# A decoder layer on one core: weight buffers laid out by release, and the order of gate tail, evictions, splits and sums changed

## The chip, the cores and the metric

The kernel runs on one core of a Trainium2 chip. The metric is the device time of one execution in microseconds; a kernel's time is the median of its runs. The engines are TensorE (PE, matmuls), VectorE (DVE), ScalarE (ACT), GpSimd (POOL) and SyncE (SP, which here only issues DMAs); each takes its instructions in program order and stops at one whose operands or buffers are not ready.

## The reference

One decoder layer in float32 for 512 tokens of width 2048. Three groups of heads read one input projection, their outputs are normalised per head, gated and projected, and an MLP with a squared ReLU follows:

```python
proj = rms_norm(h) @ w_in
(gq, gk, gv, gg, ga, fq, fk, fv, fg, ff, mq, mg) = split(proj)
...   # gated linear attention, forgetting attention, attention to a memory
o = rms_norm(concat([gla_o, fox_o, mem_o]))          # per head
gate = concat([silu(gg), sigmoid(fg), sigmoid(mg)])
h = h + (o * gate) @ w_out                           # 2048 x 2048
u = relu(rms_norm(h) @ w_up)                         # 2048 x 8192
h = h + (u * u) @ w_down                             # 8192 x 2048
```

## The kernel before, in words

**Matmuls.** Each float32 operand is split in a high and a low part of a narrower format (the high part by a cast on ACT, the low one by a subtraction on DVE), and each product is three matmuls: high by high, high by low, low by high (`mm3`, L170 to L172). The projections of the first half (`project`, L261) go in pairs of 128 rows of the weight, `kp` 0 to 7, through the double buffers raw, hi and lo of pool `wp`. The last four groups are the gates gg0, gg1, fg and mg (L645 on).

**The gate tail.** After a gate's projection, for each of four banks: z by DVE (L656), log-sigmoid as Abs, Exp, Ln on ACT and one DVE operation (L352 to L355), Exp on ACT (L658), and the product with the heads, DVE, L661. `block_sums` (L611) then makes the sums s1 to s4 of the quarters of the result. These seven blocks are the left operands: `left0` (A11) and `left3` (S1) are split at once into buffers of their own; the others go through DRAM tiles `oo` (POOL's DMAs, L673) and are fetched by SP (L606) and split (L601, L602) once the attention's buffers are given back. `left4` is S2, `left5` S3, `left6` S4, `left1` A12, `left2` A22.

**The second half.** w_out is two multiplies (out0, out1), w_up eight (up0 to up7) and w_down eight (dn0_0 to dn3_1). Each is a seven-product scheme of Strassen and Winograd: products p in the order 1, 5, 6, 3, 7, 2, 4, each of four steps q. A product's left operand is one of the seven blocks, its right operand a block of the weight or a difference of blocks. Raw weights come in 1 MB tiles `raw` from a ring of six (`wr`, loaded by SP, L710); differences are taken in place on DVE (L717); for each q ACT casts a half tile (L755) and DVE makes the low part (L756), both into a ring of four `hl` tiles (`wm`). Twelve matmuls use one `hl` tile. In out0 the first eight steps are taken as 10, 11, 12, 50, 51, 52, 13, 53 (first digit the product).

**Banks and evictions.** Products 1, 6, 7 and 4 add to one pair of PSUM banks, 5 and 3 to another; after each product the bank is read out before the next product adds to it. In w_out, DVE adds it to a tile x, loaded by SP (L795, L806); in w_up and w_down ACT copies it (z L942, m L987) or DVE adds. Blocks of the new h are turned by PE (L828) and scaled by ACT (L831), and `operands` makes their sums (hs, L615 to L621), which are the left operands of w_up: through DRAM tiles `uo` for the first half, directly split for the second.

**What sets the order.** The code is written in one sequence, and a scheduler orders each engine's instructions by priority; `tc.high_priority(offset=...)` moves what stands in it ahead. Splits and differences of weights have an offset of 3000 (`AHEAD`), block loads of x 300; evictions and the gate tail have none. Rings of buffers decide when a load may start: a tile of a ring waits for the last reader of whatever lay in its place.

## Time and profile before

| | us |
|---|---|
| median of 3 runs | 2209.56 (2207.89 to 2209.83) |
| profiled execution, its time | 2212.55 |
| profiled execution, its span | 2210.8 |
| PE busy | 2151.7 (97%) |
| DVE busy | 1534.9 (69%) |
| ACT busy | 1076.9 (49%) |
| GpSimd busy | 115.2 (5%) |

The span runs from the first to the last instruction on the engines; 1.75 us of the profiled execution lie around it. Busy shares are means over the whole program. The projections and the attention fill the first 741 us, w_out runs to about 945 us, w_up to about 1600 and w_down to the end. The views used are the busy shares of the page, the windows view (busy time, granted clock and DMA rate of a stretch), the timeline of one engine (start, duration, operation, idle time before it and what released it) and the list of waits.

### The profile page before, as it was taken

How to read it: one execution, taken by the hardware profiler on the slowest of the kernel's cores; microseconds unless marked ns; L12 is line 12 of the kernel's file. 1: busy time of each engine (PE TensorE's matmuls, PEld its weight loads, DVE VectorE, ACT ScalarE, POOL GpSimd, SP SyncE). 2: the span in 40 equal slices, each digit the busy share in tenths (PEclk: the TensorE clock that was granted, in tenths of full speed). 3: DMA queues.
4: the chain of work that ended last, by engine and by line, in shares of the span. 5: the costliest groups of instructions: out<-in, count | busy, mean ns of one | idle time of the engine just before them, and what ended most of it. 6: DMA issues, size and time to landing. Idle time of an engine off the chain costs nothing. (4 is left out here: it accounts for less than half of the span.)

```text
span 2210.8 us, 25318 instructions
## 1 busy us (share of the span) xinstructions
PE 2151.7 (97%) x9842; PEld 1750.4 (79%) x9842; DVE 1534.9 (69%) x1714; ACT 1076.9 (49%) x1469; POOL 115.2 (5%) x187
## 2 busy tenths in 40 slices
PE   8999999999999878999999999999999999999999
PEld 7777778777778657878888888888878888788787
DVE  5264775247576678787687677778868868767775
ACT  5233232345554445555555545555645546546443
POOL 2000000000001001000000000000010000000000
PEclk9999999999999989999999999999999999999999
DMA  5222112225134365614534433534676777668554
GB/s 192 83 77 76 50 56 80 73 91 171 60 106 145 140 221 213 233 68 157 176 130 150 171 143 126 189 143 182 237 211 187 221 200 210 190 196 267 149 189 133
DMA packets 72131, 336.61 MB, mean 152 GB/s; under 512 B 8377, under 2 KB 10425, under 8 KB 49994
## 3 DMA queue, kind: packets, MB, share of 16 engines
q1 hardware_dynamic: 53162, 267.35, 34.8%
q0 software_dynamic: 18848, 67.64, 11.3%
q8 instruction: 77, 1.26, 0.2%
q14 instruction: 44, 0.36, 0.0%
HBM read 263.13 MB, written 71.83 MB: 152 GB/s over the span
## 5 line engine op out<-in xcount | busy, mean ns | idle before, releaser
L755 ACT CAST hl_up<-raw_up 128x1024 fp32r<-128x1024 f32 x224 | 235.8, 1053 | 283.3 <-PE acc_up L172 258.9
L756 DVE TENSOR_TENSOR hl_up<-raw_up,hl_up 128x1024 fp32r<-128x1024 f32 x224 | 273.2, 1222 | 137.1 <-ACT hl_up L755 136.8
L755 ACT CAST hl_dn<-raw_dn 128x1024 fp32r<-128x1024 f32 x224 | 235.5, 1053 | 240.1 <-PE acc_dn L172 185.9
L756 DVE TENSOR_TENSOR hl_dn<-raw_dn,hl_dn 128x1024 fp32r<-128x1024 f32 x224 | 270.7, 1221 | 101.1 <-ACT hl_dn L755 100.7
L717 DVE TENSOR_TENSOR raw_dn<-raw_dn,raw_dn 128x2048 f32<-128x2048 f32 x64 | 145.9, 2287 | 16.1 <-DMA raw_dn<-in_w_down_dram 15.8
L717 DVE TENSOR_TENSOR raw_up<-raw_up,raw_up 128x2048 f32<-128x2048 f32 (+1 forms) x65 | 146.4, 2253 | 2.1 <-DMA raw_up<-in_w_up_dram 1.9
L755 ACT CAST hl_out<-raw_out 128x1024 fp32r<-128x1024 f32 x56 | 58.4, 1052 | 71.6 <-PE acc_out L172 57.2
L756 DVE TENSOR_TENSOR hl_out<-raw_out,hl_out 128x1024 fp32r<-128x1024 f32 x56 | 67.8, 1222 | 32.2 <-ACT hl_out L755 32.0
L988 POOL DMA_DIRECT2D hd<-m x48 | 41.6, 874 | 508.5 <-ACT m L987 508.5
L987 ACT COPY m<-acc_dn 128x512 f32<-128x512 f32 x96 | 55.6, 584 | 8.7 <-PE acc_dn L172 8.7
L171 PE MATMUL gg<-alo_x,hi_gg 128*128 128x512 f32 x128 | 52.9, 414 | 0.0
L171 PE MATMUL acc_up<-hl_up,left0h 128*128 128x512 f32 x128 | 50.3, 393 | 1.9 <-DVE hl_up L756 1.9
L170 PE MATMUL acc_dn<-hl_dn,left4h 128*128 128x512 f32 x128 | 50.0, 390 | 2.2 <-ACT m L987 2.2
L171 PE MATMUL acc_dn<-hl_dn,left4h 128*128 128x512 f32 x128 | 50.1, 391 | 1.9 <-DVE hl_dn L756 1.9
L170 PE MATMUL gg<-ahi_x,hi_gg 128*128 128x512 f32 x128 | 51.8, 405 | 0.0
L170 PE MATMUL acc_up<-hl_up,left0h 128*128 128x512 f32 x128 | 50.7, 397 | 1.1 <-ACT hl_up L755 1.1
L171 PE MATMUL gv<-lo_gv,ahi_x 128*128 128x512 f32 x128 | 51.7, 404 | 0.0
L172 PE MATMUL gv<-hi_gv,alo_x 128*128 128x512 f32 x128 | 51.6, 403 | 0.0
L170 PE MATMUL acc_up<-hl_up,left4h 128*128 128x512 f32 x128 | 49.9, 390 | 1.6 <-ACT z L942 1.6
L172 PE MATMUL gg<-ahi_x,lo_gg 128*128 128x512 f32 x128 | 51.3, 402 | 0.0
L171 PE MATMUL acc_dn<-hl_dn,left3h 128*128 128x512 f32 x128 | 50.3, 393 | 0.9 <-DVE hl_dn L756 0.9
L170 PE MATMUL acc_up<-hl_up,left3h 128*128 128x512 f32 x128 | 50.8, 397 | 0.0
(545 smaller groups left out, 6088.2 us busy)
## 6 DMA issues: line engine op xcount, KB each, us to landing
raw_up<-in_w_up_dram SPq DMA_DIRECT2D x64, 1024.0 KB, 4.8
raw_dn<-in_w_down_dram SPq DMA_DIRECT2D x64, 1024.0 KB, 6.9
hd<-m POOLq DMA_DIRECT2D x48, 512.0 KB, 7.5
raw_out<-in_w_out_dram SPq DMA_DIRECT2D x16, 1024.0 KB, 4.9
op<-u POOLq DMA_DIRECT2D x32, 512.0 KB, 3.1
op<-s POOLq DMA_DIRECT2D x24, 512.0 KB, 2.9
raw_gv<-in_w_in_dram SPq DMA_DIRECT2D x16, 512.0 KB, 3.4
raw_mem<-in_w_mem_dram SPq DMA_DIRECT2D x16, 512.0 KB, 3.7
```

The source lines that it names most:

```text
L170: T.matmul(ps, lhsT=ah, rhs=bh, start=start, stop=False, skip_group_check=on)
L171: T.matmul(ps, lhsT=ah, rhs=bl, start=False, stop=False, skip_group_check=on)
L172: T.matmul(ps, lhsT=al, rhs=bh, start=False, stop=stop, skip_group_check=on)
L717: V.tensor_sub(dst[:, cs], a[:, cs], b[:, cs])
L755: A.copy(hi, part)
L756: V.tensor_sub(lo, part, hi.bitcast(F32))
L987: A.copy(st[:, t * 512 : t * 512 + 512], acc[t])
L988: nc.gpsimd.dma_start(dst, st.rearrange("p (t n) -> p t n", t=2), accum_op=ALU.add)
```

## The change

The weight buffers and the `hl` tiles get fixed places instead of rings: a raw tile has one of six tags, by block and half, and a group of four blocks starts one tag further on; `hl` tiles count through four tags. The last projection, mg, goes through its weight pairs in the order 0, 7, 6, ... 1, in the other pool of banks. The high part and three quarters of the low part of S2 (`left4`) get a resident pool `third`; for the first three gates it is split in place and only the last quarter goes through DRAM, into a tile `left4m`. The tail of mg, with its sums and DMAs, is put at an offset of 6000, the evictions of all products likewise (`urgent`), and the fetches of the left operands for w_out at 1000. The x tiles are loaded from `inside` at the first step of a product. The sums of `operands` for f = 0, 1 and 2 go to GpSimd. A renewed left operand is fetched one product later. The number of matmuls is the same.

The diff, cut to its core:

```diff
+    third = ctx.enter_context(tc.tile_pool(name="third", bufs=1))
...
-    def project(*groups, turned=False, first=False, bank=gbank):
-
+    def project(*groups, turned=False, first=False, bank=gbank, order=range(NK // 2)):
+
+        first_k, last_k = 2 * order[0], 2 * order[-1] + 1
...
-        for kp in range(NK // 2):
+        for kp in order:
...
+    CUT = 1536
+    high = {i: bigt([128, 2048], f"left{i}h", FR) for i in (A11, S1)}
+    low = {i: [bigt([128, 2048], f"left{i}l", FR)] for i in (A11, S1)}
+    high[S2] = third.tile([128, 2048], FR, name=f"left{S2}h")
+    low[S2] = [third.tile([128, CUT], FR, name=f"left{S2}l")]
...
-    def block_sums(a11, a12, a21, a22, temp):
+    def block_sums(a11, a12, a21, a22, temp, eng=V):
...
+        def add(dst, a, b, op):
+            eng.tensor_tensor(dst, a, b, op=op)
...
-        ps = project(group, turned=True, bank=gbank if n < 3 else abank)
+        last = n == 3
+
+        ps = project(
+            group, turned=True, bank=abank if last else gbank, order=(0, 7, 6, 5, 4, 3, 2, 1) if last else range(NK // 2)
+        )
+        finish_heads = ExitStack()
+        if last:
+            finish_heads.enter_context(tc.high_priority(offset=2 * AHEAD))
...
-            if i in left:
-                hi, lo = (halves(v[:, cs]) for v in left[i])
+            if i in (A11, S1) or i == S2 and not last:
+                hi, lo = halves(high[i][:, cs]), halves(lower(i, cs))
...
-    wm = ctx.enter_context(tc.tile_pool(name="wm", bufs=4, reuse_waits="tile"))
-    wr = ctx.enter_context(tc.tile_pool(name="wr", bufs=6, reuse_waits="tile"))
+    wm = ctx.enter_context(tc.tile_pool(name="wm", bufs=1, reuse_waits="tile"))
+    wr = ctx.enter_context(tc.tile_pool(name="wr", bufs=1, reuse_waits="tile"))
...
+    low[S2].append(ap.tile([128, 2048 - CUT], FR, name=f"left{S2}m"))
...
+    def urgent():
+        return tc.high_priority(offset=2 * AHEAD)
...
-            raw = wr.tile([128, 2048], F32, tag="raw", name=f"raw_{name}_{r}{c}{s}")
+
+            slot = {(0, 0): 0, (0, 1): 1, (1, 1): 2, (1, 0): 2}[r, c] + group
+            raw = wr.tile([128, 2048], F32, tag=f"raw{slot % 3}{s}", name=f"raw_{name}_{r}{c}{s}")
...
-                both = wm.tile([128, 2048], FR, tag="hl", name=f"hl_{name}_{p}{q}")
+                both = wm.tile([128, 2048], FR, tag=f"hl{turns['hl'] % 4}", name=f"hl_{name}_{p}{q}")
+                turns["hl"] += 1
...
-            tasks.append((0, lambda: fetch(i, cs, src)))
+            tasks.append((1, lambda: fetch(i, cs, src)))
...
-            r, c = {1: (0, 0), 2: (0, 0), 6: (0, 1), 3: (0, 1), 5: (1, 1), 7: (1, 1), 4: (1, 0)}[p]
-            if p in (1, 6, 5, 4):
-                z[r, c] = block(r, c)
-            for t in range(2):
-                v = z[r, c][:, t * 512 : t * 512 + 512]
-                V.tensor_add(v, v, acc[t])
+            r, c = WHERE[p]
+            with urgent():
+                for t in range(2):
+                    v = z[r, c][:, t * 512 : t * 512 + 512]
+                    V.tensor_add(v, v, acc[t])
...
+            parts = block_sums(
+                h0[:, :512], h0[:, 512:], h1[:, :512], h1[:, 512:], temps.get, G if f < 3 else V
+            )
...
         def inside(p, q):
+            if q == 0 and p in (1, 6, 5, 4):
+                block(*WHERE[p])
...
-        for cs in (slice(0, 1536), slice(1536, 2048)):
-            fetch(i, cs, out_op[i][:, cs])
+        for cs in (slice(0, 1536), slice(1536, 2048))[i == S2 :]:
+            with tc.high_priority(offset=1000):
+                fetch(i, cs, out_op[i][:, cs])
...
-            evict(p, acc)
+            with urgent():
+                evict(p, acc)
```

What the change moves is seen in each engine's list of instructions. On ACT, at the end of mg and the start of out0 (ee_mg is the gate tail, hl_out_10 the cast of product 1, step 0), before:

```order
L658 ACTIVATE ee_mg_5841<-ee_mg_5841 128x512
L354 ACTIVATE ee_mg_5850<-ee_mg_5850,wide 128x512
L755 CAST hl_out_10_5969<-raw_out_000_5963 128x1024
L755 CAST hl_out_11_5984<-raw_out_000_5963 128x1024
L658 ACTIVATE ee_mg_5850<-ee_mg_5850 128x512
L353 ACTIVATE ee_mg_5859<-ee_mg_5859 128x512
L755 CAST hl_out_12_5999<-raw_out_001_5965 128x1024
L354 ACTIVATE ee_mg_5859<-ee_mg_5859,wide 128x512
L670 CAST left0h<-o 128x512
L658 ACTIVATE ee_mg_5859<-ee_mg_5859 128x512
L755 CAST hl_out_50_6022<-raw_out_000_5963 128x1024
L755 CAST hl_out_51_6037<-raw_out_000_5963 128x1024
```

and now:

```order
L355 ACTIVATE ee_mg_5869<-ee_mg_5869 128x512
L702 CAST left0h<-o 128x512
L690 ACTIVATE ee_mg_5860<-ee_mg_5860 128x512
L356 ACTIVATE ee_mg_5869<-ee_mg_5869,wide 128x512
L801 CAST hl_out_10_5975<-raw_out_000_5969 128x1024
L690 ACTIVATE ee_mg_5869<-ee_mg_5869 128x512
L801 CAST hl_out_11_5992<-raw_out_000_5969 128x1024
L801 CAST hl_out_12_6007<-raw_out_001_5971 128x1024
L702 CAST left3h<-s_mg 128x512
L801 CAST hl_out_50_6030<-raw_out_000_5969 128x1024
L801 CAST hl_out_51_6047<-raw_out_000_5969 128x1024
L801 CAST hl_out_52_6062<-raw_out_001_5971 128x1024
```

The tail's activations, but for the last Exp, stand ahead of hl_out_10 now, and left3h of the last gate ahead of hl_out_50.

On DVE, in out0, around the first eviction (x_00 from bank acc_out_1; L717 and L762 are differences of raw tiles, L756 and L802 low parts), before:

```order
L756 TENSOR_TENSOR hl_out_61_6127<-raw_out_000_5963,hl_out_61_6127 128x1024
L717 TENSOR_TENSOR raw_out_011_6017<-raw_out_111_6109,raw_out_011_6017 128x2048
L756 TENSOR_TENSOR hl_out_62_6142<-raw_out_001_5965,hl_out_62_6142 128x1024
L615 TENSOR_TENSOR s_mg<-o 128x512
L621 TENSOR_TENSOR s_mg<-o 128x512
L617 TENSOR_TENSOR s_mg<-s_mg,o 128x512
L671 TENSOR_TENSOR left3l<-s_mg,left3h 128x512
L619 TENSOR_TENSOR s_mg<-o,s_mg 128x512
L806 TENSOR_TENSOR x_00_6082<-x_00_6082,acc_out_1_0_5967 128x512
L756 TENSOR_TENSOR hl_out_63_6157<-raw_out_001_5965,hl_out_63_6157 128x1024
L806 TENSOR_TENSOR x_00_6082<-x_00_6082,acc_out_1_1_5968 128x512
L806 TENSOR_TENSOR x_11_6102<-x_11_6102,acc_out_5_0_6020 128x512
```

and now:

```order
L802 TENSOR_TENSOR hl_out_52_6062<-raw_out_001_5971,hl_out_52_6062 128x1024
L802 TENSOR_TENSOR hl_out_13_6077<-raw_out_001_5971,hl_out_13_6077 128x1024
L762 TENSOR_TENSOR raw_out_000_5969<-raw_out_110_6112,raw_out_000_5969 128x2048
L762 TENSOR_TENSOR raw_out_001_5971<-raw_out_011_6025,raw_out_001_5971 128x1024
L621 TENSOR_TENSOR left4m<-left4m,left4h 128x512
L802 TENSOR_TENSOR hl_out_60_6118<-raw_out_000_5969,hl_out_60_6118 128x1024
L802 TENSOR_TENSOR hl_out_53_6095<-raw_out_001_5971,hl_out_53_6095 128x1024
L802 TENSOR_TENSOR hl_out_61_6135<-raw_out_000_5969,hl_out_61_6135 128x1024
L762 TENSOR_TENSOR raw_out_001_5971<-raw_out_111_6115,raw_out_001_5971 128x2048
L762 TENSOR_TENSOR raw_out_011_6025<-raw_out_111_6115,raw_out_011_6025 128x2048
L853 TENSOR_TENSOR x_00_5990<-x_00_5990,acc_out_1_0_5973 128x512
L853 TENSOR_TENSOR x_00_5990<-x_00_5990,acc_out_1_1_5974 128x512
```

The sums s_mg have gone ahead of this place; the eviction x_00 now stands ahead of hl_out_62, behind two differences of 128x2048.

On SP, where the x tiles of out1 are loaded (x_10 is still out0's; the next x_00, x_11 and x_01 are out1's; left0l and left3l are fetched from the sums of the new h), before:

```order
L710 DMA raw_out_111_6680<-in_w_out_dram 128x2048
L795 DMA x_10_6481<-in_x_dram 128x1024
L606 DMA left0l<-uo_5926 128x1024
L606 DMA left3l<-uo_5929 128x1024
L795 DMA x_00_6600<-in_x_dram 128x1024
L795 DMA x_11_6672<-in_x_dram 128x1024
```

and now:

```order
L753 DMA raw_out_111_6685<-in_w_out_dram 128x2048
L842 DMA x_10_6442<-in_x_dram 128x1024
L842 DMA x_00_6530<-in_x_dram 128x1024
L626 DMA left0l<-uo_5935 128x1024
L842 DMA x_11_6633<-in_x_dram 128x1024
L842 DMA x_01_6703<-in_x_dram 128x1024
L626 DMA left3l<-uo_5938 128x1024
```

x_00 of out1 stands ahead of left0l and left3l, and all its x tiles ahead of left3l.

## Rows read from the trace of the kernel before

**Rows 1.** The page: engines' shares, and low parts of w_out (busy, mean ns).

```profile
PE 2151.7 (97%) x9842; PEld 1750.4 (79%) x9842; DVE 1534.9 (69%) x1714; ACT 1076.9 (49%) x1469; POOL 115.2 (5%) x187
...
L756 DVE TENSOR_TENSOR hl_out<-raw_out,hl_out 128x1024 fp32r<-128x1024 f32 x56 | 67.8, 1222 | 32.2 <-ACT hl_out L755 32.0
```

**Rows 2.** Windows: length, busy PE, PEld, DVE, ACT, POOL; PE clock; DMA; GB/s.

```profile
700.00:750.00 50.00, 43.48 (x187) 35.19 (x186) 25.05 (x33) 23.84 (x38) 3.12 (x5) 0.95 0.35 129
750.00:800.00 50.00, 35.58 (x131) 27.60 (x131) 41.95 (x39) 21.93 (x24) 3.26 (x6) 0.81 0.60 228
800.00:850.00 50.00, 46.48 (x206) 38.19 (x206) 35.57 (x35) 25.34 (x39) 5.43 (x10) 0.97 0.63 216
850.00:900.00 50.00, 42.75 (x187) 34.96 (x187) 39.96 (x36) 21.97 (x29) 4.34 (x8) 0.93 0.44 162
...
950.00:1000.00 50.00, 45.31 (x193) 36.16 (x192) 42.96 (x47) 26.29 (x39) 0.53 (x1) 0.97 0.22 77
```

**Rows 3.** Timeline of PE: start, length, operation [idle before it and its releaser].

```profile
747.93 1.22 PE L170 MATMUL acc_out<-hl_out,left0h 128*128 128x512 f32 x2 [6.48 <-ACT hl_out L755]
...
777.55 0.80 PE L170 MATMUL acc_out<-hl_out,left3h 128*128 128x512 f32 x1 [8.05 <-ACT left3h L670]
...
789.59 0.79 PE L170 MATMUL acc_out<-hl_out,left4h 128*128 128x512 f32 x1 [6.37 <-ACT left4h L601]
...
816.88 0.59 PE L170 MATMUL acc_out<-hl_out,left5h 128*128 128x512 f32 x1 [3.52 <-DVE x L806]
...
884.00 0.77 PE L170 MATMUL acc_out<-hl_out,left4h 128*128 128x512 f32 x1 [7.25 <-DVE x L806]
...
955.58 0.50 PE L171 MATMUL acc_up<-hl_up,left0h 128*128 128x512 f32 x1 [1.94 <-DVE hl_up L756]
```

**Rows 4.** PE's waits over the span: us in total, times, longest.

```profile
PE acc_dn L171 <- DVE hl_dn L756: 2.7, 5, 0.9
PE acc_dn L170 <- ACT m L987: 2.2, 1, 2.2
...
PE ot L642 <- DVE o L638: 1.7, 1, 1.7
```

**Rows 5.** Timeline of ACT, at the start and in the middle of out0.

```profile
740.17 0.63 ACT L352 ACTIVATE ee_mg<-z_mg 128x512 f32<-128x512 f32 x1 [8.74 <-DVE z_mg L656]
...
746.85 1.98 ACT L755 CAST hl_out<-raw_out 128x1024 fp32r<-128x1024 f32 x2
...
824.25 1.05 ACT L755 CAST hl_out<-raw_out 128x1024 fp32r<-128x1024 f32 x1 [1.68 <-PE acc_out L172]
826.96 1.05 ACT L755 CAST hl_out<-raw_out 128x1024 fp32r<-128x1024 f32 x1 [1.66 <-PE acc_out L172]
```

**Rows 6.** Timeline of DVE in out0.

```profile
761.68 5.62 DVE L717 TENSOR_TENSOR raw_out<-raw_out,raw_out 128x2048 f32<-128x2048 f32 x3
...
776.17 0.68 DVE L615 TENSOR_TENSOR s_mg<-o 128x512 f32<-128x512 f32 x1
...
816.05 2.48 DVE L806 TENSOR_TENSOR x<-x,acc_out 128x512 f32<-128x512 f32 x4
```

**Rows 7.** Timeline of SP's queue: first issue, time to the last of them.

```profile
741.25 3.10 SPq L710 DMA_DIRECT2D raw_out<-in_w_out_dram  x6
744.40 35.76 SPq L795 DMA_DIRECT2D x<-in_x_dram  x3
...
877.64 1.79 SPq L795 DMA_DIRECT2D x<-in_x_dram  x3
```

**Rows 8.** DMA, 740 to 800: rate in 40 slices, one issue (KB, us to landing).

```profile
GB/s 0 87 366 426 431 426 431 431 415 431 437 396 418 208 0 0 0 0 0 0 0 0 0 0 0 30 320 147 303 374 434 406 412 221 318 391 427 397 415 128
...
oo<-s_mg POOLq DMA_DIRECT2D x3, 256.0 KB, 4.5
```

**Rows 9.** Timelines of POOL and of DVE in the attention.

```profile
274.14 1.46 POOL L459 TENSOR_TENSOR qk<-qTs,kTs 128x512 f32<-128x512 f32 x1 [40.75 <-PE lp L447]
...
274.96 1.19 DVE L444 TENSOR_TENSOR e<-e,kTs 128x512 f32<-128x512 f32 x1
```

More of the change, by code (lines that the diff above doesn't have):

```diff
@@ L591, in hybrid_layer, with lower, pieces @@
         )
-    left = {i: [bigt([128, 2048], f"left{i}{p}", FR) for p in "hl"] for i in (A11, S1)}
-    out_op = {i: dram.tile([128, 2048], F32, name=f"oo_{i}") for i in range(7) if i not in left}
+    CUT = 1536
[3 more added lines that the diff above has]
+    low[S2] = [third.tile([128, CUT], FR, name=f"left{S2}l")]
+    out_op = [dram.tile([128, 2048], F32, name=f"oo_{i}") for i in range(7)]
+    def lower(i, cs):
+        if i != S2:
+            return low[i][0][:, cs]
+        if cs.start < CUT:
+            assert cs.stop <= CUT
+            return low[i][0][:, cs]
+        return low[i][1][:, cs.start - CUT : cs.stop - CUT]
+    def pieces(i, cs):
+        if i == S2 and cs.start < CUT < cs.stop:
+            return [slice(cs.start, CUT), slice(CUT, cs.stop)]
+        return [cs]
     def split_left(i, cs, src):
-        hi, lo = (v[:, cs] for v in left[i])
-        A.copy(hi, src)
-        V.tensor_sub(lo, src, hi.bitcast(F32))
+        A.copy(high[i][:, cs], src)
+        V.tensor_sub(lower(i, cs), src, high[i][:, cs].bitcast(F32))
     def fetch(i, cs, src):
-        nc.sync.dma_start(left[i][1][:, cs].bitcast(F32), src)
+        for c in pieces(i, cs):
+            nc.sync.dma_start(lower(i, c).bitcast(F32), src[:, c.start - cs.start : c.stop - cs.start])
     def resplit(i, cs):
-        split_left(i, cs, left[i][1][:, cs].bitcast(F32))
-    def block_sums(a11, a12, a21, a22, temp):
+        for c in pieces(i, cs):
+            split_left(i, c, lower(i, c).bitcast(F32))
+    def block_sums(a11, a12, a21, a22, temp, eng=V):
         s1, s2, s4, s3 = (temp(v) for v in ("s1", "s2", "s4", "s3"))
+        def add(dst, a, b, op):
+            eng.tensor_tensor(dst, a, b, op=op)
         yield A11, a11
-        V.tensor_add(s1, a21, a22)
+        add(s1, a21, a22, ALU.add)
         yield S1, s1
-        V.tensor_sub(s2, s1, a11)
+        add(s2, s1, a11, ALU.subtract)
         yield S2, s2
-        V.tensor_sub(s4, a12, s2)
+        add(s4, a12, s2, ALU.subtract)
         yield S4, s4
-        V.tensor_sub(s3, a11, a21)
+        add(s3, a11, a21, ALU.subtract)
         yield S3, s3
@@ L685, in hybrid_layer @@
     ap = ctx.enter_context(tc.tile_pool(name="ap", bufs=1, side="right", reuse_waits="tile"))
-    wm = ctx.enter_context(tc.tile_pool(name="wm", bufs=4, reuse_waits="tile"))
-    wr = ctx.enter_context(tc.tile_pool(name="wr", bufs=6, reuse_waits="tile"))
+    wm = ctx.enter_context(tc.tile_pool(name="wm", bufs=1, reuse_waits="tile"))
+    wr = ctx.enter_context(tc.tile_pool(name="wr", bufs=1, reuse_waits="tile"))
     mp = ctx.enter_context(tc.tile_pool(name="mp", bufs=STAGES, reuse_waits="tile"))
-    for i in (S2, S4, S3, A12, A22):
-        left[i] = [ap.tile([128, 2048], FR, name=f"left{i}{p}") for p in "lh"][::-1]
+    for i in (S4, S3, A12, A22):
+        low[i] = [ap.tile([128, 2048], FR, name=f"left{i}l")]
+        high[i] = ap.tile([128, 2048], FR, name=f"left{i}h")
+    low[S2].append(ap.tile([128, 2048 - CUT], FR, name=f"left{S2}m"))
     ssq = const.tile([128, NT, 4], F32, name="ssq")
@@ L759, in multiply @@
                     j = 2 * q + kk
-                    ah, al = (a[:, j * 256 + u * 128 : j * 256 + u * 128 + 128] for a in left[OPERAND[p]])
+                    ts = slice(j * 256 + u * 128, j * 256 + u * 128 + 128)
+                    ah, al = high[OPERAND[p]][:, ts], lower(OPERAND[p], ts)
                     cs = slice(kk * 512, kk * 512 + 512)
@@ L793, in block @@
             with tc.high_priority(offset=300):
-                v = stage(f"x_{n}_{r}{c}")
-                nc.sync.dma_start(v.rearrange("p (t n) -> p t n", t=2), x[r, 2 * n + c])
-            return v
+                z[r, c] = stage(f"x_{n}_{r}{c}")
+                nc.sync.dma_start(z[r, c].rearrange("p (t n) -> p t n", t=2), x[r, 2 * n + c])
+        WHERE = {1: (0, 0), 2: (0, 0), 6: (0, 1), 3: (0, 1), 5: (1, 1), 7: (1, 1), 4: (1, 0)}
         def after(p, acc):
@@ L838, in operands @@
         def operands(f, h0, h1):
+            cs = slice(f * 512, f * 512 + 512)
             st = [stage(f"hs_{f}_{i}") for i in range(2)]
             temps = dict(s1=st[0][:, :512], s2=st[0][:, 512:], s4=st[1][:, :512], s3=st[1][:, 512:])
-            cs = slice(f * 512, f * 512 + 512)
-            for i, src in block_sums(h0[:, :512], h0[:, 512:], h1[:, :512], h1[:, 512:], temps.get):
+            parts = block_sums(
+                h0[:, :512], h0[:, 512:], h1[:, :512], h1[:, 512:], temps.get, G if f < 3 else V
+            )
+            for i, src in parts:
                 if not n:
@@ L959, in inside @@
             if (p, q) == (1, 1):
-                with tc.high_priority(offset=300):
-                    rest()
+                rest()
                 ss = const.tile([128, NT], F32, name="ss_h")
@@ L976, in after @@
             rest()
-            evict(p, acc)
+            with urgent():
+                evict(p, acc)
             renew(p, read_down(c + 1) if n and not final else None)
```

8 lines of the change are left out of this document (6 added, 2 removed).

## The prediction

> **What bounds the kernel now.** I read the page's busy shares first: TensorE (PE) works 97% of the span, the next engine (DVE) 69% [rows 1]. So a change that leaves the matmuls alone, as this one does (9,494 matmul rows on PE before and after), can only win what PE loses in gaps and at the low clock after them. Where these are, the windows view tells [rows 2]: in each stretch of 50 us, PE's busy time times the granted clock is the work it did at full speed, and what lacks to 50 is lost. 700 to 750: 50 - 43.48 x 0.95 = 8.7 us; 750 to 800: 50 - 35.58 x 0.81 = 21.2; 800 to 850: 4.9; 850 to 900: 10.2; 950 to 1000: 6.0. Together 51 us, 2.3% of the span; the rest of the w_up and w_down stages runs nearly without gaps. That is the most there is to win here.
>
> The timeline of PE in those stretches names each gap and its releaser [rows 3]: 6.48 us before the first product of w_out (the cast hl_out), 8.05 (left3h), 6.37 (left4h), 3.52 and 7.25 (evictions x), and 1.94 at the start of w_up. The list of PE's waits adds a lone 2.2 us at the w_down stage and 1.7 at the head transposes [rows 4]. What the reader is to see is that none of these is a lack of engine time: each is an order. SP issues the six 1 MB loads raw_out only at 741.25, as the last matmul of mg ends, and only then come x and left4l, 744.40 to 780.26 [rows 7]. DVE runs three block differences at 761.68 and reaches the sum s_mg, which left3h waits for, at 776.17; the four evictions at 816.05 stand in the same queue [rows 6].
>
> **A, the start of w_out.** Four casts and activations more stand ahead of hl_10 on ACT (16 where there were 12). The twelve took from 740.17 to 746.85 [rows 5], 0.557 us each, so the cast moves to 749.1 and PE's start, 1.08 behind it, from 747.93 to 750.2: 2.2 us are lost here. The loads are no longer the reason: three of the six now go out before mg's last pair of rows, and the remaining 3 MB at about 426 GB/s [rows 8] are in by 749. Then DVE decides. From the low part of q 10 (751.4) to that of q 50 it issues three 128x1024 (1.15 us each, a little under the mean of 1222 ns in [rows 1], as neighbours overlap), six 128x512 at 0.62 (a quarter of 2.48 in [rows 6]) and the three differences for 5.62 [rows 6]: 12.8 us, so PE goes on at 764.2. One q takes PE 2.71 us (two casts that each wait for PE stand that far apart, 824.25 and 826.96 [rows 5]); three of them and 2.5 us of low clock end at 760.8, which leaves a new idle of 3.4. The five q up to 53 end at 777.8. The sum s_mg and left3h are done by 756, so the gap of 8.05 is gone. q 60 adds to the bank of product 1 and waits for the eviction x_00. Ahead of that on DVE, after hl_50: six 128x1024 (6.9), three 128x2048 and one 128x1024 difference (7.7), one 128x512 and the two evictions (1.9), 16.5 us, to 780.7. Its other condition is x_00 in place, and the x loads now stand behind the left fetches on SP: left4m waits for oo of s2 (summed at 755, DMA 4.5 us [rows 8]: 759.5), then 4.75 MB at 426 GB/s are 11.7 us: 771 to 773, in time. So PE starts q 60 at 780.7 where it was 789.59 [rows 3]: **8.9 us won**. Bounds: 0, if the fetches or casts of left6 and left5, which stand ahead of hl_60 and hl_53 on ACT, come as late as left4h does now; 12, if q 60 follows q 53 without a gap.
>
> **B, the gap at 816.88.** On DVE the eviction of x_01 now stands ahead of hl_32; before, the splits up to hl_73 and two differences preceded it. PE has all of product 3 (four q, 10.8 us) before it needs the bank. The whole loss of that window goes: **4.9 us** (bounds 3.5, the idle alone, and 4.9).
>
> **C, the gap at 884.00.** x_1_00 was issued at 877.64 [rows 7], behind left3l, which waited on SP for a sum on its way through DRAM. It now stands ahead of left0l and left3l; what it waits for is a stage buffer, free when GpSimd has done the four sums of f=0. With 1.46 us for a 128x512 on GpSimd [rows 9] and the DMA issues between them I get about 850, more than 10 us ahead of need. **10.2 us**, bounds 0 (buffer late) and 10.2.
>
> **D, sums on GpSimd and the start of w_up.** Twelve sums go from DVE (0.68 us, [rows 6]) to GpSimd; the nearest row for what they cost there is the one 128x512 product on that engine, 1.46 us [rows 9]. Those of f=0 and 1 feed DRAM copies and are hidden. For f=2, four splits wait on them on ACT and DVE, ahead of the first casts hl_up: four sums now last 5.7 us instead of 2.7, so hl_up_11 may come up to 4 us later, while DVE, which sets the pace there (the 1.94 of [rows 3]), is relieved of 2.7 us. I take **0**, bounds -8 (4 us late, with as much again for the low clock and the queue behind) and +6 (the window's whole loss).
>
> At these sums the Trainium skill speaks against the change: "SBUF — State Buffer", section "Who interferes with whom", says that a DVE instruction with two SBUF inputs and a GpSimd instruction that reads SBUF exclude each other for a whole instruction. The trace agrees: while GpSimd's product ran from 274.14 to 275.60, the DVE product that began at 274.96 took 1.19 us [rows 9], 0.5 over the 0.68 of its size. By that rule the twelve sums cost DVE at most 12 x 0.5 = 6 us, which counts on PE for f=2 alone, 2 us; that would leave D's value inside its bounds.
>
> **E and F.** The eviction m of [rows 4] now precedes the next cast on ACT: **2.2 us** (bounds 0 and 2.2). The transposes ot_2 and ot_3 are issued later and may lose the 1.7 of [rows 4], but whether they meet another wait there I can't see: **0**, up to 1.7. At no cost I put S2's in-place split for the first three groups (a cast and a subtraction of 128x512 for each, under running projections), the two-piece fetch of left4 (one more DMA issue) and the ring order of the weight buffers in steady state. Their cover is the slack of a cast: four hl buffers, a cast of about 1 us and a low part of 1.2 against three q of 2.71; without it each would cost its own length at each product.
>
> **The sum.** 8.9 + 4.9 + 10.2 + 0 + 2.2 + 0 = 26.2 us. The profiled execution lies 2.99 us above the median of the runs (2212.55 and 2209.56); taken off the first it gives 2186.4, off the median 2183.4. I predict 2183.
>
> **Rivals.** *The gap only moves.* The casts of left6 and left5 wait for their fetches with hl_60 and hl_53 behind them, or x_00 comes late; A is 0 and 17.3 us remain: 2192. For it: 8 MB pass one queue in order, and DMA was full here for 14 us already [rows 8]. Against it: my times leave x_00 seven us. Chance 0.17.
> *GpSimd holds up x_1_00 and w_up.* D is -8 and C 0: 8.0 us remain, 2201.5. For it: 1.46 us where DVE takes 0.68, and the stretched 1.19 of [rows 9]. Against it: GpSimd is otherwise idle there. Chance 0.13.
> *All is covered.* q 60 follows at once (12), w_up starts without loss (6), the transposes too (1.7): 37.0 us, 2172.6. For it: both remaining gaps are 3 us by a sum of many small terms. Chance 0.17.
> *Slower.* The evictions now stand ahead of a cast at each product's end, on ACT or DVE. If the cast that is pushed back then comes too late, all 112 products of w_up and w_down pay. Today's five waits of that kind cost 2.7 us, 0.54 each [rows 4]: 60 us, and 34 more than before after the gains, 2244. It decides from 0.27 us a product, where it eats the 26 us and the 4.4 that can be measured. Against it stands the slack named above, 8.1 us for a push of 1.2. Chance 0.06.
> *It does not do what it says*, since each freed wait is followed by another at the same place: under 4.4 us, about 2208. Chance 0.04.
>
> **How the numbers follow.** The forecast (2177 to 2189) has 0.43. Faster by over 0.2%, 4.4 us, about what a measurement of this kernel can tell from no change: 0.43 + 0.17 + 0.17 and most of the GpSimd case, 0.88. Within it: 0.04 and the rest of that case, 0.06. Slower: 0.06. The range leaves out the last two cases and the ends of their neighbours: from all covered (2172.6, less the 2.7 us of small waits of w_down [rows 4]) to the GpSimd case (2201.5, and 1.4 us, B's other bound): 2169 to 2203.
>
> **What will show it.** In the new trace, PE's first q of w_out at about 750, not earlier; an idle of 3 us before q 50, released by a low part, and of 3 before q 60, released by x; no wait for left3h or left4h; no gap at products 7 of the first pair and 6 of the second (816.88 and 884.00 now); GpSimd sums of about 1.4 us, and the wait at w_up's start of about 5 us as now. I am wrong if PE waits for left6h or left5h, if x_00 lands after 780, if x_1_00 is issued after 865, or if small idles stand at every product of w_up.

## The result, and the profile after it

The changed kernel takes **2189.61 us** (median of 4 runs, 2187.03 to 2191.86), the kernel before beside it 2209.69: ratio 0.990, 95% interval 0.9869 to 0.9931, faster by 1.0%. The forecast was 2183.0 with 2169 to 2203; side and range held, and the time lies 6.6 us above the forecast. The profiled execution took 2189.32 us, with a span 23.2 us shorter than before's 2210.8. Three executions ran at a granted clock of 0.56 or 0.64 (two of the kernel called Together below, 3604 and 3609 us, and one of the last, 3128 us), and the times below leave them out. The page's shares answer to [rows 1]:

```profile
PE 2147.0 (98%) x9842; PEld 1748.0 (80%) x9842; DVE 1535.0 (70%) x1708; ACT 1076.3 (49%) x1475; POOL 132.8 (6%) x196
```

The engines do what they did, and GpSimd 17.6 us more. What changed is in the windows (length, busy PE, PEld, DVE, ACT, POOL; PE clock; DMA; GB/s), beside [rows 2]:

```profile
700.00:750.00 50.00, 41.31 (x178) 33.44 (x178) 25.56 (x34) 24.46 (x38) 2.73 (x5) 0.94 0.51 187
750.00:800.00 50.00, 45.90 (x184) 36.78 (x184) 47.57 (x43) 25.96 (x27) 3.11 (x5) 0.92 0.51 190
800.00:850.00 50.00, 50.00 (x238) 41.77 (x237) 41.28 (x33) 29.43 (x50) 17.64 (x21) 1.00 0.75 270
850.00:900.00 50.00, 48.78 (x219) 40.13 (x219) 45.05 (x40) 25.99 (x34) 6.37 (x8) 1.00 0.59 203
900.00:950.00 50.00, 43.91 (x199) 35.58 (x198) 45.10 (x42) 32.95 (x54) 8.18 (x6) 0.95 0.29 105
950.00:1000.00 50.00, 50.00 (x225) 41.41 (x225) 33.61 (x37) 25.20 (x32) 1.07 (x2) 0.98 0.46 160
```

The 9,494 matmul rows of the prediction stand in no view shown here; the page counts 9842 instructions on PE in both kernels.

Read as before (50 less busy PE times clock), the stretches lose 11.2, 7.8, 0, 1.2, 8.3 and 1.0 us: 29.5 in place of 51. The start of w_out is a little worse, 750 to 900 is nearly clean, and the start of w_up (now in 900 to 950) loses more than it did. PE's timeline names what is left, beside [rows 3]:

```profile
748.31 1.22 PE L171 MATMUL acc_out<-hl_out,left0h 128*128 128x512 f32 x2 [8.65 <-ACT hl_out L801]
...
761.64 0.73 PE L171 MATMUL acc_out<-hl_out,left0h 128*128 128x512 f32 x2 [1.36 <-ACT hl_out L801]
...
777.88 0.50 PE L171 MATMUL acc_out<-hl_out,left4h 128*128 128x512 f32 x1 [2.74 <-DVE x L853]
...
860.95 0.50 PE L172 MATMUL acc_out<-hl_out,left4h 128*128 128x512 f32 x1 [1.22 <-DVE hl_out L802]
...
940.34 0.50 PE L172 MATMUL acc_up<-hl_up,left3h 128*128 128x512 f32 x1 [1.70 <-DVE hl_up L802]
...
947.49 0.80 PE L171 MATMUL acc_up<-hl_up,left4h 128*128 128x512 f32 x1 [4.35 <-ACT z L996]
...
1590.56 0.77 PE L171 MATMUL acc_dn<-hl_dn,left4h 128*128 128x512 f32 x1 [2.65 <-ACT m L1041]
```

The waits in out0 for left3h and left4h and the gap before product 7 are gone, and of the 7.25 us before product 6 of out1, 1.22 are left, for a low part. q 60 of out0 waits 2.74 us for the eviction x_00, as forecast (3). The wait for z in up0 has grown to 4.35 us; in the kernel before it was 1.62:

```profile
973.38 0.50 PE L170 MATMUL acc_up<-hl_up,left4h 128*128 128x512 f32 x1 [1.62 <-ACT z L942]
```

Between these gaps the same matmuls stand at the same distances in both traces, so the difference in start of one matmul, taken where PE has the same work behind it in both, tells what was won up to it:

| matmul | before | after | won so far | of it here |
|---|---|---|---|---|
| mg, first | 697.76 | 695.98 | 1.8 | 1.8 (F and before) |
| out0, q 60 | 789.59 | 777.88 | 11.7 | 9.9 (A) |
| out1, first | 853.78 | 836.59 | 17.2 | 5.5 (B) |
| out1, product 3 | 897.22 | 871.78 | 25.4 | 8.2 (C) |
| up0, product 3 | 984.39 | 960.76 | 23.6 | -1.8 (D) |
| dn0_0, product 3 | 1624.81 | 1603.16 | 21.6 | -2.0 (E) |
| end of the span | 2210.8 | 2187.6 | 23.2 | 1.6 (small waits) |

### The profile page after: what moved, and what is told of

It is laid out like the page before. It is cut to its first block, busy times and chain, and to the rows that moved or that the text cites. A ratio compares the mean times of both kernels' runs of the same rounds, so it can differ in the third digit from the quotient of the medians.

```text
span 2187.6 us, 25319 instructions
## 1 busy us (share of the span) xinstructions
PE 2147.0 (98%) x9842; PEld 1748.0 (80%) x9842; DVE 1535.0 (70%) x1708; ACT 1076.3 (49%) x1475; POOL 132.8 (6%) x196
## 5 line engine op out<-in xcount | busy, mean ns | idle before, releaser
L802 DVE TENSOR_TENSOR hl_up<-raw_up,hl_up 128x1024 fp32r<-128x1024 f32 x224 | 273.8, 1227 | 139.5 <-ACT hl_up L801 139.4
L802 DVE TENSOR_TENSOR hl_dn<-raw_dn,hl_dn 128x1024 fp32r<-128x1024 f32 x224 | 270.7, 1221 | 97.3 <-ACT hl_dn L801 96.6
L762 DVE TENSOR_TENSOR raw_dn<-raw_dn,raw_dn 128x2048 f32<-128x2048 f32 x64 | 146.2, 2286 | 17.4 <-DMA raw_dn<-in_w_down_dram 17.2
L762 DVE TENSOR_TENSOR raw_up<-raw_up,raw_up 128x2048 f32<-128x2048 f32 (+1 forms) x65 | 146.3, 2252 | 0.3
L802 DVE TENSOR_TENSOR hl_out<-raw_out,hl_out 128x1024 fp32r<-128x1024 f32 x56 | 69.7, 1264 | 15.3 <-ACT hl_out L801 15.2
L171 PE MATMUL acc_up<-hl_up,left4h 128*128 128x512 f32 x128 | 50.9, 398 | 4.3 <-ACT z L996 4.3
L172 PE MATMUL acc_dn<-hl_dn,left0h 128*128 128x512 f32 x128 | 50.3, 393 | 1.4 <-DVE hl_dn L802 1.3
L172 PE MATMUL acc_up<-hl_up,left4h 128*128 128x512 f32 x128 | 50.7, 396 | 0.0
L171 PE MATMUL gv<-hi_gv,ahi_x 128*128 128x512 f32 x128 | 50.6, 395 | 0.0
```

Source lines behind the costliest of these rows:

```text
L171: T.matmul(ps, lhsT=ah, rhs=bh, start=start, stop=False, skip_group_check=on)
L172: T.matmul(ps, lhsT=ah, rhs=bl, start=False, stop=False, skip_group_check=on)
L762: V.tensor_sub(dst[:, cs], a[:, cs], b[:, cs])
L802: V.tensor_sub(lo, part, hi.bitcast(F32))
```

## The experiments

The theory was that of the forecast: order, not engine time, makes the gaps, and each part of the change lifts its own wait. The question is which part lifts which. Times are set against the changed kernel's 2189.6, ratios against the kernel before in the same session (2212.45, 2212.27, 2211.98 and 2209.94).

**The tail of mg without its priority.**

```diff
-            finish_heads.enter_context(tc.high_priority(offset=2 * AHEAD))
+            pass
```

> The changed kernel, but the gate tail of mg keeps the ordinary priority; everything else of the change stays. Theory (the order of the tail's sums on DVE is what removes the wait for left3h): the cast hl_out of q 10 comes about 2 us earlier than the 747.23 of the changed kernel, and PE waits again some 8 us for left3h and a few for left4h; q 60 starts 8 to 11 us later, time 2197 to 2201. Rival (the weight loads that are out early are what won the start of w_out): 2187 to 2191, no wait for left3h.

2197.85 us, ratio 0.9942 (0.9919 to 0.9965): 8.2 slower, as expected. The first product starts 2.8 earlier (745.53), and in PE's timeline the wait for left3h and the gap before product 7 are back:

```profile
775.16 0.80 PE L171 MATMUL acc_out<-hl_out,left3h 128*128 128x512 f32 x1 [7.84 <-ACT left3h L702]
...
780.75 0.55 PE L171 MATMUL acc_out<-hl_out,left4h 128*128 128x512 f32 x1
...
806.59 0.77 PE L171 MATMUL acc_out<-hl_out,left5h 128*128 128x512 f32 x1 [3.74 <-DVE x L853]
```

Yet q 60 (the left4h row) is only 2.9 us later than in the changed kernel, not back at 789.59. The tail alone doesn't carry A.

**The evictions without theirs.**

```diff
-        return tc.high_priority(offset=2 * AHEAD)
+        return ExitStack()
```

> The changed kernel, but no eviction has a raised priority; x_1_00 still stands ahead of left3l on SP. Theory: the eviction of x_01 is again behind splits, so term B comes back, 3.5 to 5 us, and C stays won; up0 and dn0_0 differ by 2 us either way: 2192 to 2197. Rival 1 (the priority of evictions is worth nothing, since ACT and DVE have slack): 2188 to 2191. Rival 2 (raised evictions push back casts in w_up and w_down, and the plain ones are better there): 2180 to 2187.

2206.92 us, 0.998 (0.9967 to 0.9993): 17.3 slower and 10 above the upper end of what was expected. The miss is at q 60, in PE's timeline:

```profile
789.08 0.79 PE L171 MATMUL acc_out<-hl_out,left4h 128*128 128x512 f32 x1 [14.12 <-DVE x L853]
```

and its reason in DVE's, where the low parts of four left operands go ahead of x_00:

```profile
779.26 2.35 DVE L621 TENSOR_TENSOR left6l<-left6l,left6h 128x1536 fp32r<-128x1536 f32 x2
...
786.07 2.35 DVE L621 TENSOR_TENSOR left2l<-left2l,left2h 128x1536 fp32r<-128x1536 f32 x2
788.35 2.48 DVE L853 TENSOR_TENSOR x<-x,acc_out 128x512 f32<-128x512 f32 x4
```

In the changed kernel x_00 starts at 777.15. I take it that the splits get in front of an eviction that isn't raised because the left operands are fetched earlier; that wasn't tried alone.

**The evictions alone raised, in the kernel before.**

```diff
-            for t in range(2):
-                v = z[r, c][:, t * 512 : t * 512 + 512]
-                V.tensor_add(v, v, acc[t])
+            with urgent():
+                for t in range(2):
+                    v = z[r, c][:, t * 512 : t * 512 + 512]
+                    V.tensor_add(v, v, acc[t])
...
-            evict(p, acc)
+            with urgent():
+                evict(p, acc)
```

> The kernel before with one part of the change alone: all evictions at the raised priority. Theory (the parts depend on each other: without the tail moved up, q 60 still waits for left4h, and x_1_00 still stands behind left3l): only the gap of 3.5 us at product 7 of the first pair goes, and up0's start moves by a few us; 4 to 8 us under the kernel before. Rival (each part has a price of its own, and raised evictions are worth here the 17 us that their removal costs in the changed kernel): 15 to 18 us under the kernel before.

2196.52 us, 0.9939 (0.9922 to 0.9955): 15.8 us won of the change's 20, by one part of it. That fell on the rival's side. Nothing is won up to q 60 of out0; product 7's gap is gone, out1's q 60 waits 3.90 in place of 7.25, and the wait of 1.94 in up0 has left:

```profile
789.35 0.80 PE L170 MATMUL acc_out<-hl_out,left4h 128*128 128x512 f32 x1 [7.05 <-ACT left4h L601]
...
875.85 0.47 PE L170 MATMUL acc_out<-hl_out,left4h 128*128 128x512 f32 x1 [3.90 <-DVE x L810]
```

q 60 of out0 now tells how A is built. Raised evictions alone: 789.35, it waits for left4h. Tail and third operand without raised evictions: 789.08, for x. Raised evictions and third operand without the tail: 780.75. All: 777.88. The waits stand in series, and the last to end decides; up to this matmul neither the raised evictions nor the rest without them is worth anything. The third operand's part of it (split in place, fetched ahead) is inferred from 789.35 against 780.75, two kernels that differ in the buffers and the sums too, and wasn't undone alone.

**The weight buffers as rings again, mg's weights in their old order.**

```diff
-    wr = ctx.enter_context(tc.tile_pool(name="wr", bufs=1, reuse_waits="tile"))
+    wr = ctx.enter_context(tc.tile_pool(name="wr", bufs=6, reuse_waits="tile"))
...
-            raw = wr.tile([128, 2048], F32, tag=f"raw{slot % 3}{s}", name=f"raw_{name}_{r}{c}{s}")
+            raw = wr.tile([128, 2048], F32, tag="raw", name=f"raw_{name}_{r}{c}{s}")
```

(and likewise for `hl`, and `order` left at its default)

> The changed kernel with the weight tiles and hl tiles in plain rings again and the pairs of mg in rising order, so that all six loads of w_out are issued only as mg ends; the tail, evictions, left4 and sums stay as changed. Theory (16 operations of the tail on ACT, not the loads, set the first cast): the first matmul of w_out within 2.5 us of the 748.31 of the changed kernel, time 2188 to 2193. Rival (the early loads carry the gain): the first cast 5 to 8 us later and DVE's differences late as well, time 2196 to 2203.

2187.03 us, 0.9892 (0.9875 to 0.9909), 2.6 us faster if anything. PE's start is the same to 0.1 us (748.41, after an idle of 8.65), though SP issues the six loads about as late as before (741.25 [rows 7]):

```profile
739.56 3.08 SPq L753 DMA_DIRECT2D raw_out<-in_w_out_dram  x6
```

So what the change's description begins with, the layout by release, moves loads by up to 25 us (in the changed kernel the first goes out at 714.99) and time by nothing that these runs can tell: the wait is for a cast in ACT's queue, not for its data.

**The place of the x loads**, tried with plain and with raised evictions.

```diff
             r, c = WHERE[p]
+            if p in (1, 6, 5, 4):
+                block(r, c)
...
-            if q == 0 and p in (1, 6, 5, 4):
-                block(*WHERE[p])
```

With plain evictions:

> As the kernel without raised evictions, and the x tiles are loaded after their product again, so that x_1_00 stands behind left0l and left3l on SP as it did before the change. Theory: x_1_00 is issued only when the sum for left3l has landed, the wait of 7 us before q 60 of out1 comes back, and the time is 8 to 12 us over that of the kernel without raised evictions: 2202 to 2208. Rival (the place of x_1_00 on SP does not matter, the earlier start of the stage does): within 2 us of it.

2216.66 us, 1.002 (1.0008 to 1.0033): 9.7 over plain evictions alone, as expected, and slower than before. Out1's q 60 pays it:

```profile
883.46 0.77 PE L171 MATMUL acc_out<-hl_out,left4h 128*128 128x512 f32 x1 [11.59 <-DVE x L855]
```

With raised evictions:

> The changed kernel with raised evictions, but the x tiles are loaded at the eviction again, as before, and not at a product's first step. In the list of SP x_00 of out1 now stands behind left0l (issued at 842.72 in the changed kernel) and still ahead of left3l (854.10). Theory: the load then goes out at about 843 and lands some 4 us later, more than 10 us ahead of q 60's eviction at about 858, so with raised evictions the new place of the load is worth nothing: 2188 to 2192, as the changed kernel (2189.6), no wait for x at the start of product 6 of out1. Rival: the place is worth the whole of C however the evictions are ordered, as between the two kernels with plain evictions (10 us): 2197 to 2201, with a wait of 7 us or more for x near 866. Between them: the wait of 3.90 at 875.85 that was left in the kernel before with raised evictions, where x stood behind left3l (issued at 868.49), comes back: 2193 to 2195.

2189.89 us, 0.9906 (0.9888 to 0.9925): the same time as the changed kernel. SP's queue shows why, first with plain and then with raised evictions:

```profile
876.03 0.33 SPq L626 DMA_DIRECT2D left3l<-uo  x1
876.52 1.88 SPq L842 DMA_DIRECT2D x<-in_x_dram  x3
```

```profile
841.88 1.31 SPq L842 DMA_DIRECT2D x<-in_x_dram  x3
853.15 0.33 SPq L626 DMA_DIRECT2D left3l<-uo  x1
```

With raised evictions x is issued ahead of left3l without being placed there. The kernel before with raised evictions still had left3l first (its x loads went out at 868.49, and 3.90 us were left), so another part of the change, the later fetch of a renewed operand perhaps, lends a hand; that wasn't separated.

**All sums on DVE again.**

```diff
-                h0[:, :512], h0[:, 512:], h1[:, :512], h1[:, 512:], temps.get, G if f < 3 else V
+                h0[:, :512], h0[:, 512:], h1[:, :512], h1[:, 512:], temps.get, V
```

> The changed kernel with all sums of the new h on DVE again. Theory (the sums on GpSimd hide and cost about what they give, term D near 0): 2186 to 2193, with DVE's operations at their usual 0.68 and 1.22 us in that stretch. Rival 1 (GpSimd's sums stretch DVE's operations that overlap them, and PE pays): 2181 to 2186. Rival 2 (DVE has no room for the four sums ahead of w_up, and PE waits there again for a low part as it did before the change): 2193 to 2198, with the waits in the first 20 us of w_up.

2183.97 us, 0.9882 (0.9867 to 0.9896): **5.6 us faster** than the changed kernel, all four executions below all four of its. The theory of this run, that the sums cost about what they give, said 2186 to 2193 and missed; the time is that of its first rival. The low parts of w_out, grouped (least, median, greatest ns), in the changed kernel and then with the sums on DVE:

```profile
L802 DVE TENSOR_TENSOR hl_out<-raw_out,hl_out x56: 1209/1219/2311, 748.3 to 906.6; 128x1024 fp32r<-128x1024 f32 x56
```

```profile
L802 DVE TENSOR_TENSOR hl_out<-raw_out,hl_out x56: 1217/1220/1226, 748.1 to 904.9; 128x1024 fp32r<-128x1024 f32 x56
```

The stretched ones are those beside a GpSimd sum; without them the wait of 1.22 at 860.95 is gone, and PE is 1.7 us ahead of the changed kernel at product 3 of out1, 4.6 ahead at product 3 of up0. The 2.9 of up0 come by order: the evictions z now stand ahead of a cast on ACT, and the waits of 1.70 and 4.35 become one of 3.44:

```profile
939.83 0.79 PE L171 MATMUL acc_up<-hl_up,left3h 128*128 128x512 f32 x1 [3.44 <-ACT left3h L620]
```

**The eviction m ahead of what `rest()` issues.**

```diff
-            rest()
             with urgent():
                 evict(p, acc)
+            rest()
```

> The changed kernel; only in w_down the eviction is written ahead of the work left over from the last w_up product, so that ACT takes the two copies m ahead of the two turned activations u, and still behind the cast of q 63. Theory (ACT's order alone sets the wait of 2.65 us at the start of w_down): the wait falls by the length of the two u, to 1.5 to 1.7 us, the time by 1 to 2 us, 2187 to 2189. Rival (m waits for its stage buffer or for PE): no change of the wait.

2187.28 us, 0.9893 (0.9878 to 0.9908), as expected; 2.3 faster by the medians, with intervals that overlap; between product 3 of up0 and product 3 of dn0_0 the traces differ by 2.6. ACT's timeline in the changed kernel and then here:

```profile
1588.00 1.05 ACT L801 CAST hl_dn<-raw_dn 128x1024 fp32r<-128x1024 f32 x1 [1.67 <-PE acc_dn L173]
1588.95 1.08 ACT L938 ACTIVATE u<-ut 128x512 f32<-128x512 f32 x2
1589.91 2.05 ACT L1041 COPY m<-acc_dn 128x512 f32<-128x512 f32 x4
```

```profile
1588.45 1.05 ACT L801 CAST hl_dn<-raw_dn 128x1024 fp32r<-128x1024 f32 x1 [1.67 <-PE acc_dn L173]
1589.40 1.07 ACT L1041 COPY m<-acc_dn 128x512 f32<-128x512 f32 x2
```

A cast and two activations u stood ahead of m in the changed kernel; the two u gone, PE's wait is 1.68 in place of 2.65. That is 1.0 us; the other 1.6 are the clock in these two executions. The windows of the 5 us from the end of this wait, in the kernel before (a wait of 2.18 [rows 4]), the changed one (2.65) and this one (1.68), columns as above:

```profile
1613.00:1618.00 5.00, 4.25 (x18) 3.49 (x19) 5.00 (x5) 3.22 (x6) 3.13 (x5) 1.00 0.98 320
```

```profile
1590.00:1595.00 5.00, 4.45 (x13) 3.54 (x13) 3.96 (x4) 1.96 (x5) 3.45 (x5) 0.66 0.55 188
```

```profile
1590.00:1595.00 5.00, 4.97 (x22) 4.12 (x23) 4.91 (x5) 3.48 (x6) 3.46 (x5) 1.00 0.53 138
```

Behind the idle of 2.65 the granted clock is 0.66 in the mean of that stretch (a matmul takes 0.63 us up to 1593.26, then 0.39 to 0.40 from 1594.08), behind those of 2.18 and 1.68 it stays at 1.00. But the length of the wait doesn't settle it. In the kernel with the plain tail the same wait is as long, and the clock stays at 1.00:

```profile
1597.84 0.50 PE L171 MATMUL acc_dn<-hl_dn,left4h 128*128 128x512 f32 x1 [2.65 <-ACT m L1041]
```

```profile
1597.00:1602.00 5.00, 4.16 (x18) 3.47 (x19) 3.91 (x4) 3.30 (x6) 3.44 (x5) 1.00 0.57 193
```

From product 3 of up0 to product 3 of dn0_0 PE takes 640.4 us in the kernel before, 642.4 in the changed kernel, 640.8 with the plain tail and 639.8 here. So 1.0 us of this edit's gain is order, and the other 1.6 belong to executions in which the clock falls there.

**The first casts ahead of the tail, the differences of product 7 put back.**

```diff
-                with tc.high_priority(offset=AHEAD):
+                with tc.high_priority(offset=0 if p == 7 and name == "out0" else AHEAD):
...
-            with tc.high_priority(offset=AHEAD):
+            with tc.high_priority(offset=AHEAD * (4 if name == "out0" and p == 1 and q < 2 else 1)):
```

> The changed kernel with two orders altered in the first multiply of w_out: the casts and low parts of q 10 and q 11 ahead of the gate tail, and product 7's two differences of 128x2048 without raised priority, so that DVE makes them after the first eviction and not before it. Theory (what is left at the start of w_out is order on ACT and DVE): first matmul about 2 us earlier, at 746; q 60 at 770 to 773 where it was 777.88; time 2182 to 2186. Rival (the fetches of left4m and left6 or the x load come next): q 60 at 776 or later behind a left part, 2187 to 2192.

2188.74 us, 0.990 (0.9885 to 0.9915): no gain, where 2182 to 2186 was expected. The number is the rival's, but not for its reason: no left part holds q 60 up. The first wait is 6.48 again and q 60 starts at 773.18 without one, 4.7 us earlier (6.5 counted from mg, which came 1.8 later in this execution). Then product 7's own differences are too late, first for an eviction between them, then for its low part, as DVE's timeline and PE's show:

```profile
795.00 2.29 DVE L762 TENSOR_TENSOR raw_out<-raw_out,raw_out 128x2048 f32<-128x2048 f32 x1
797.21 0.68 DVE L853 TENSOR_TENSOR x<-x,acc_out 128x512 f32<-128x512 f32 x1
797.81 2.29 DVE L762 TENSOR_TENSOR raw_out<-raw_out,raw_out 128x2048 f32<-128x2048 f32 x1
```

```profile
797.94 0.66 PE L875 MATMUL ht<-ident,x 128*128 128x128 f32 x4 [2.60 <-DVE x L853]
...
801.28 0.79 PE L172 MATMUL acc_out<-hl_out,left5h 128*128 128x512 f32 x1 [1.83 <-DVE hl_out L802]
```

The wait moved one product on: 0 was too low a priority, 3000 too high.

**Together:** sums on DVE, m first, the two casts early and product 7's differences of out0 at an offset of 200.

```diff
-                with tc.high_priority(offset=AHEAD):
+                with tc.high_priority(offset=200 if p == 7 and name == "out0" else AHEAD):
```

> The changed kernel with four orders altered: sums of the new h on DVE; m ahead of the turned activations at the start of w_down; casts of q 10 and 11 of the first w_out multiply ahead of the gate tail; and product 7's two differences there behind the first eviction and the split of left5, but ahead of those of left1 and left2 (in early_casts they came behind these, and PE waited 2.6 and 1.8 us at product 7). Theory (each wait that is left has a price of its own, on DVE and ACT): 5.6 from the sums, 1.5 from m and 4 to 6 from the start of w_out, 2176 to 2180. Rival (the next wait takes most of it): 2181 to 2185.

2179.3 and 2180.0 us, 0.9851 (0.9832 to 0.9871), inside the expected 2176 to 2180. No trace of it is read here. Two ways on from it, both in up0: the first sum of the last four raised,

```diff
+            with tc.high_priority(offset=ahead if dst is s1 else 0):
+                eng.tensor_tensor(dst, a, b, op=op)
```

> As combined, but the first sum of the last quarter of h, which left3h waits for at the start of w_up, has a raised priority on DVE. Theory (PE's wait of 3.4 us for left3h at w_up is that sum's place): the wait goes, 2 to 4 us under combined. Rival (DVE is full there, and ACT takes z behind the cast of q 63 again): the wait for left3h is replaced by one of 2 to 4 us for z, within 2 us of combined.

2175.23 us, 0.9834 (0.9818 to 0.9851), 4.4 under Together: the wait for left3h (3.44 with the sums on DVE alone) isn't there, and one of 2.64 for z stands in its place, which was the rival's sign, though the time is the theory's or better. And product 7's differences at 200 in up0 too,

```diff
-                with tc.high_priority(offset=200 if p == 7 and name == "out0" else AHEAD):
+                with tc.high_priority(offset=200 if p == 7 and name in ("out0", "up0") else AHEAD):
```

> As combined, but product 7's two differences are taken late in the first multiply of w_up too, which takes 4.5 us of DVE's work out of its first product. Theory (DVE's queue sets that start): PE's waits in the first 30 us of w_up fall from about 3.4 to under 2 us, 2 to 4 us under combined. Rival (ACT's order sets it, z stands behind the cast of q 63): a wait of 2 to 4 us for z, within 2 us of combined.

2172.34, 2173.14 and 2173.34 us, ratio **0.9821** (0.9805 to 0.9838): the best here, 16 us below the changed kernel and 6.5 under Together, where 2 to 4 were expected; the start of w_up lost its wait as told, and where the rest comes from can't be told without a trace of Together. The waits of over 1 us from 740 on:

```profile
746.62 1.22 PE L171 MATMUL acc_out<-hl_out,left0h 128*128 128x512 f32 x2 [6.48 <-ACT hl_out L801]
...
810.79 0.50 PE L173 MATMUL acc_out<-hl_out,left1l 128*128 128x512 f32 x1 [1.77 <-DVE left1l L621]
...
936.94 0.50 PE L171 MATMUL acc_up<-hl_up,left4h 128*128 128x512 f32 x1 [1.68 <-ACT z L996]
...
1576.78 0.50 PE L171 MATMUL acc_dn<-hl_dn,left4h 128*128 128x512 f32 x1 [1.68 <-ACT m L1041]
```

## Why the prediction was right, point by point

**What bounds the kernel** held: 21.5 of the 23.2 us come from the 51 us that the windows showed as lost, by moving waits, with every engine but GpSimd as busy as before.

**A, 8.9 forecast, 9.9 measured.** Its steps came as told: PE's first product 0.4 us later than before (750.2 forecast; 748.31, since mg itself had come 1.8 earlier), and 2.74 before q 60. The idle forecast as 3.4 before q 50, released by a low part, was one of 1.36 between steps of product 1 and 5, released by a cast. Where the working was silent is on which edit it rests: the 16.5 us of DVE work that it counted to x_00 hold only for a raised eviction. Unraised, x_00 is 11 us later.

**B, 4.9 and 5.5.** A little over its upper bound: in the kernel before, product 7 came 3.7 us late and ran 1.7 longer at the low clock, 5.4 where the window's shares gave 4.9. It hangs on the raised eviction: the gap goes when that part alone is made in the kernel before. That it returns without the tail (3.74 at 806.59) I didn't foresee, and why it does wasn't traced.

**C, 10.2 and 8.2.** The time was near, and one reason for it wrong. The step that put it down to the load's new place fell: with raised evictions the load may stand where it stood (2189.89), and only with plain ones does the place give 10 us. Of the 2.0 us that lack, most is the new wait of 1.22 at 860.95, behind low parts stretched by GpSimd's sums: with the sums on DVE the same stretch wins 9.8.

**D, 0 forecast, -1.8 at up0, and 5.6 for the sums on GpSimd as a whole.** The mis-sized term. Its bounds, -8 to +6, held it, but the value in the middle was a choice between two unknowns. The sums of f=1, which I had told of as hidden, are the ones whose stretch PE paid for (1.7), and not priced at all was that the order on ACT and DVE at up0 depends on where the sums run, the larger part (2.9). The rule cited for it holds. In the timelines of DVE and then GpSimd:

```profile
845.15 2.31 DVE L802 TENSOR_TENSOR hl_out<-raw_out,hl_out 128x1024 fp32r<-128x1024 f32 x1
847.38 3.38 DVE L762 TENSOR_TENSOR raw_out<-raw_out,raw_out 128x2048 f32<-128x2048 f32 x1
850.68 0.68 DVE L853 TENSOR_TENSOR x<-x,acc_out 128x512 f32<-128x512 f32 x1
```

```profile
826.83 1.28 POOL L637 TENSOR_TENSOR hs<-ht 128x512 f32<-128x512 f32 x1 [0.93 <-ACT ht L878]
...
844.94 1.44 POOL L637 TENSOR_TENSOR hs<-ht 128x512 f32<-128x512 f32 x1 [5.31 <-ACT ht L878]
846.34 2.27 POOL L637 TENSOR_TENSOR hs<-ht,ht 128x512 f32<-128x512 f32 x1
...
849.14 2.77 POOL L637 TENSOR_TENSOR hs<-hs,ht 128x512 f32<-128x512 f32 x1
```

GpSimd's first sum ends at 846.38; DVE's low part ends at 847.46, 1.1 us after it where it takes 1.22 alone. GpSimd's second ends at 848.61, 1.15 after that (alone 1.28); DVE's difference at 850.76, 2.15 after that (alone 2.28). They take turns. The Trainium skill, "SBUF — State Buffer", "Who interferes with whom", says just this, and that a DVE instruction with at most one input in SBUF, outside the modes that use two ports, stays free: the eviction x, whose other input lies in PSUM, took its usual 0.68 at 850.68 beside a GpSimd sum. The 2 us on PE that were estimated from that page came as 1.7, but from the sums of f=1 and not of f=2.

**E, 2.2 forecast, -2.0 measured.** The step that failed is "the eviction m now precedes the next cast on ACT". I took that from the diff and didn't read the order there: the cast and two u stand ahead of m, and the wait grew from 2.18 to 2.65. So 0.5 us were lost by order where 2.2 were to be won. The other 1.5 of the 2.0 are the clock, which fell behind the wait in this execution and not behind the same 2.65 with the plain tail: that part is this execution's, not the order's price. With m ahead of u the stretch won 0.6.

**F, 0 forecast, 1.8 won** up to mg: the idles before the two transposes went from 1.66 and 1.01 to 1.08 and 0.60, which is 1.0; the rest lies earlier and wasn't traced. Executions scatter here: of the eleven traces with the changed first half, ten have mg's first matmul at 695.0 to 696.5 and one at 697.76, against 697.76 and 697.49 in the two with the old one.

**The sum.** The terms made 26.2, the two executions differ by 23.2, which is 3.0 too much: C, D and E gave 8.0 less, A, B and F 3.4 more, and small waits 1.6 more. The misses partly cancelled: without the 5.0 won beyond what was told, the time would have been about 2195, still in the range. The other half of the miss is the subtraction: the terms came from an execution 2.99 us above its median, and I took them off the median all the same. The alternative named beside it, 2186.4, takes them off that execution, and the changed kernel's own profiled execution lies at its median (2189.32 and 2189.61). A profiled execution's gaps are that execution's gaps.

**The rivals.** *The gap only moves* didn't happen in this kernel; it did in the one with early casts. *GpSimd holds up* was half right, with the wrong victim: x_1_00 was issued in time (843.15), and DVE paid. *All is covered* needs more edits, and then comes: 2173, where it said 2172.6. That the numbers meet is partly chance, since the gains come from edits that this case didn't know. *Slower* by raised evictions didn't come: the small waits for low parts in w_down fell from 2.7 us in five to 1.3 in three.

```profile
PE acc_dn L172 <- DVE hl_dn L802: 1.3, 3, 0.7
```

The account by parts: raised evictions alone 15.8 us, and the tail of mg 8.2 on top of the rest, against 5.6 lost by sums on GpSimd, make 18.4 of 20.1. These three were measured beside different neighbours, so the sum is a rough account and no proof. Beside raised evictions the layout of the buffers and the place of the x loads add nothing that these runs can tell from zero; the in-place split of S2, the raised fetches and the later fetch of a renewed operand weren't undone alone.

## What to carry to other kernels

Where several waits stand in series ahead of one matmul, undo each edit alone and do each alone: the same edit was worth 11 us or nothing by what stood beside it, so a gain can't be handed out among edits from one pair of traces. A read-out of a bank that the next product needs gained most here when it got a priority above the work that only prepares, and a new priority is read off the order of the instructions, not the diff. Moving elementwise sums with both inputs in SBUF from a busy DVE to an idle GpSimd wasn't relief here, since the two take turns. And what an idle on PE costs beyond its own length isn't to be read from one pair of traces.
